# Two output weights prepared earlier, in other tiles, and the first gated values loaded ahead

## The chip, the cores and the metric

The kernel runs on one core of a Trainium2 chip, in one launch. The metric is the device time in microseconds (us), the median over runs. Times of single instructions and waits come from one execution that the hardware profiler recorded; times on its clock are counted from the start of its span.

## The reference

The program computes a decoder of two layers on a sequence of 1024 rows of 1024 numbers, all in float32. One layer reads its input once, mixes it in two parallel branches, and adds the result to the input:

```python
h = layer_norm(x) * (1 + scale) + shift        # scale, shift, gate from the condition
u, v, z_a, q, k, val, z_b, q_idx, k_idx, w_idx = split(h @ w_in)
y_a = silu(z_a) * spatial_gating_unit(u, v)    # 512 columns: the top half
y_b = silu(z_b) * sparse_attention(...)        # 512 columns: the bottom half
y = concatenate([y_a, y_b]) @ w_out
x = layer_norm(ALPHA * x + gate * y, ln_g, ln_b)
```

The attention has 8 heads of 64 and one shared key and value; an indexer scores all earlier keys of a query, and the softmax goes over the best 256 of them.

## The kernel before

The two layers run one after the other. In a layer the normalised input is laid out transposed (features on partitions), and split into a high and a low part. The two parts are 16 tiles of the pool "h" (128 x 1024 each): eight for the first half of the rows and eight for the second. A projection of 128 output columns and 512 rows is 24 matmuls (line 358): eight slices of the input, each as high times high, high times low, low times high. The layer does its projections in pairs, in an order that the list `specs` gives: indexer queries, v, q, then u, z_a, u, z_a, and last z_b twice. The gated values of the first branch, y_a, are made in four tiles of the pool "ya" (lines 501 to 504) and stored in DRAM when their second z_a projection is done. The z_b projections go to DRAM as zs (lines 514 and 515). Beside the projections VectorE (DVE) selects the keys.

After the last projection come the weights of the output projection. `load_wout` prepares 512 rows of w_out (part 0 is the top half, for y_a, part 1 the bottom half, for y_b), in four slices. Each slice is 512 KB that goes through one of two tiles "wr":

```python
nc.sync.dma_start(raw, ...)                     # line 728, SP
tensor_tensor(raw, raw, gate, op=ALU.mult)      # line 729, DVE or POOL
nc.scalar.activation(hi, raw, AF.Copy)          # line 731, ACT
tensor_tensor(lo, raw, hi, op=ALU.subtract)     # line 732, POOL or DVE
```

The high and low parts lie in tiles "h" as well, so a slice's results can be written only when the last projection has read the input that lay there. The raw tile is free for the next load when the low part is done.

Then comes attention in 16 steps, a step being 4 heads of one block of 128 queries. `att_soft` forms the scores (line 685), the running maximum and masked scores on DVE (686), the exponential on ACT (691) and the scaling on POOL (694); `att_pv` transposes the probabilities (705), splits them (708, 709) and multiplies them by the values (710, 711). Probabilities lie in tiles of "ya" and "w", which `PTAGS` names in turn. Between these steps other work is fitted in by a count of instructions: `out_top` loads an x row and a block of y_a (`load_top`, whose load is line 109 and whose split into high and low is lines 311 on ACT and 312 on POOL) and multiplies it by the top weights (line 747). `merge_top` does so when the bottom half is computed with it, and `out_bottom` adds the bottom half, the layer norm and the store.

The order in which instructions are issued on each engine is fixed when the program is built: a scheduler with a timeline of its own puts them in order, and on the chip each engine takes its instructions strictly in that order and waits for the semaphores of each. SP's order is the order in which loads and stores are issued. The scheduler can move a later instruction of an engine ahead of an earlier one, so what stands next to what can't be told from the source alone.

What the steps below touch: `load_wout` with its loads (728), products (729), copies (731) and subtractions (732); `out_top` and `load_top` with lines 109, 311 and 312; the last of the `specs`; `PTAGS`; and the TensorE line 747. In the changed kernel the same lines stand one or two further down (358 is 359, 311 is 312, 685 is 686, 728 is 730, 731 is 733, 747 is 749).

## Time and profile before

| | |
|---|---|
| median of three runs | 1181.41 us (1180.64 to 1185.3) |
| profiled execution, its own time | 1184.14 us |
| its span | 1182.4 us |
| mean granted TensorE clock | 0.977 |
| PE busy | 1109.5 us, 94% of the span |
| DVE busy | 838.2 us, 71% |
| POOL busy | 575.8 us, 49% |
| ACT busy | 512.2 us, 43% |

The profiled execution is 1.74 us longer than its span. The page's busy shares are means over stages that have different limits: PE's projections, stages where DVE is the fuller engine, and short stretches in which every engine waits. Where the time goes in one place is read from the timeline of that place, which gives for each group of instructions its start, its length, and, in brackets, the idle time of the engine before it and what ended it. The granted clock is a share of full speed, 1.00 being 2.4 GHz.

### The profile page before, as it was taken

Reading aid. Unit: us, or ns where it says so; the run is one execution under the profiler, and the core shown is the slowest. Engines: PE = TensorE matmul, PEld = TensorE weight load, DVE = VectorE, ACT = ScalarE, POOL = GpSimd, SP = SyncE. Lnnn points to the kernel's source line nnn. Section 1 sums busy time; section 2 is a strip of 40 time slices with the busy share of each in tenths; the row PEclk is TensorE's granted clock in tenths of the full one; section 3 lists DMA queues with packets and bytes.
Section 4 is the critical chain, followed back from the end, with each engine's and each line's share of the span. In section 5 each row is a group of like instructions: output and inputs, shape, how many; then the busy total and the mean of one; then the engine's idle time right before and its main releaser. Section 6 shows DMA issues by size and latency. Waiting matters only on the chain.

```text
span 1182.4 us, 16568 instructions
## 1 busy us (share of the span) xinstructions
PE 1109.5 (94%) x5460; PEld 883.6 (75%) x5460; DVE 838.2 (71%) x1884; ACT 512.2 (43%) x988; POOL 575.8 (49%) x485
## 2 busy tenths in 40 slices
PE   5889999999989799989988999999999989999997
PEld 0468888777768688867666788888778877787885
DVE  6775757889869356689975447579985737878775
ACT  0343555221122445466764526552222146667561
POOL 1464311566432666365766532114654457565653
PEclk9989999999989799999998999999999999999999
DMA  8935420378742664331322453213724345132311
GB/s 260 286 94 160 142 72 26 127 244 237 228 130 81 204 188 143 108 99 63 99 89 73 116 152 121 58 57 114 249 90 152 98 141 198 54 102 78 117 36 63
DMA packets 127057, 152.11 MB, mean 129 GB/s; under 512 B 17396, under 2 KB 94580, under 8 KB 126968
## 3 DMA queue, kind: packets, MB, share of 16 engines
q1 hardware_dynamic: 126968, 151.03, 40.5%
q8 instruction: 43, 0.70, 0.2%
q14 instruction: 46, 0.38, 0.1%
HBM read 111.40 MB, written 35.40 MB: 124 GB/s over the span
## 4 chain that ended last, share of the span: by engine, by line
PE 53%; DVE 8%; DMA 3%; issue 2%; POOL 2%; ACT 1%; SPq 0%; DVEq 0%; ACTq 0%; POOLq 0%
PE pacc L358 22%; PE pacc L747 14%; PE ps L685 4%; PE ppt L705 4%; PE po L711 3%; PE po L710 2%; PE ppt L535 2%; PE ps L535 1%; POOL h L732 1%; DVE ga L709 1%; DVE ya L686 1%; DVE w L686 1%; PE po L451 1%; DMA gc<-ya 1%; DVE gb L717 1%
## 5 line engine op out<-in xcount | busy, mean ns | idle before, releaser
L358 PE MATMUL pacc<-h,w 128*128 128x512 f32 (+2 forms) x2304 | 542.5, 389 | 6.9 <-ACT gc L501 6.4
L358 PEld LDWEIGHTS pacc<-h,w 128*128 128x128 f32 (+1 forms) x2304 | 420.0, 187 | 103.0 <-ACT gc L501 10.1
L312 POOL TENSOR_TENSOR w<-wr,w 128x512 fp32r<-128x512 f32 (+1 forms) x100 | 135.0, 1366 | 211.7 <-ACT w L311 203.0
L747 PE MATMUL pacc<-h,gc 128*128 128x512 f32 x768 | 199.6, 405 | 13.4 <-ACT gc L311 12.1
L747 PEld LDWEIGHTS pacc<-h,gc 128*128 128x128 f32 x768 | 145.1, 194 | 43.3 <-ACT gc L311 13.0
L542 DVE SCALAR_TENSOR_TENSOR sc<-gc,wi,sc 128x384 f32<-128x384 f32 (+3 forms) x140 | 97.4, 740 | 56.6 <-ACT gc L537 54.0
L311 ACT ACTIVATE w<-wr 128x512 fp32r<-128x512 f32 (+1 forms) x100 | 56.8, 602 | 154.4 <-PE pacc L358 95.0
L709 DVE TENSOR_TENSOR ga<-ppt,ga 128x512 fp32r<-128x512 f32 x144 | 97.0, 684 | 20.7 <-ACT ga L708 20.1
L685 PE MATMUL ps<-kd,q 128*128 128x512 f32 (+4 forms) x384 | 104.1, 368 | 7.1 <-DVE mx L686 6.5
L708 ACT ACTIVATE ga<-ppt 128x512 fp32r<-128x512 f32 x144 | 82.7, 592 | 38.6 <-PE ppt L705 37.9
L377 POOL TENSOR_TENSOR ga<-ga,ga 128x512 fp32r<-128x512 f32 (+2 forms) x40 | 52.7, 1324 | 83.6 <-ACT ga L376 80.4
L685 PEld LDWEIGHTS ps<-kd,q 128*128 128x128 f32 x384 | 64.2, 192 | 23.8 <-DVE mx L686 17.4
L694 POOL TENSOR_SCALAR w<-w,rd 128x256 f32<-128x256 f32 (+6 forms) x77 | 61.4, 801 | 40.8 <-DVE rd L693 24.4
L691 ACT ACTIVATE w<-w,mx 128x256 f32<-128x256 f32 (+6 forms) x77 | 60.6, 787 | 35.5 <-DVE mx L686 34.9
L705 PE MATMUL ppt<-ident,w 128*128 128x128 f32 x349 | 74.1, 275 | 0.5 <-POOL w L694 0.5
L248 POOL TENSOR_TENSOR rs<-rs,mhalf 128x1 f32<-128x1 f32 x48 | 30.2, 638 | 86.4 <-DVE rs L247 85.8
L710 PE MATMUL po<-ga,vv 128*128 128x512 f32 x144 | 61.9, 430 | 9.1 <-DVE gb L717 5.7
L550 DVE TENSOR_SCALAR_CACHE_REDUCE junkd<-sc,sv 128x384 int8<-128x384 f32 (+2 forms) x72 | 67.8, 942 | 1.7
L711 PE MATMUL po<-ga,vv 128*128 128x512 f32 x144 | 63.1, 438 | 4.1 <-DVE ga L709 3.9
L694 POOL TENSOR_SCALAR ya<-ya,rd 128x256 f32<-128x256 f32 (+6 forms) x51 | 40.8, 801 | 52.3 <-DVE rd L693 30.4
L537 ACT ACTIVATE gc<-ppt 128x384 f32<-128x384 f32 (+3 forms) x96 | 47.8, 526 | 40.2 <-PE ppt L535 35.8
L705 PE MATMUL ppt<-ident,ya 128*128 128x128 f32 x227 | 58.0, 275 | 1.4 <-DVE modT L235 1.4
(197 smaller groups left out, 1729.9 us busy)
## 6 DMA issues: line engine op xcount, KB each, us to landing
wr<-in_w_in SPq DMA_DIRECT2D x50, 512.0 KB, 4.4
r<-in_w_ada SPq DMA_DIRECT2D x32, 512.0 KB, 4.7
q<-q SPq DMA_DIRECT2D x112, 128.0 KB, 3.2
q<-ga SPq DMA_DIRECT2D x48, 256.0 KB, 2.2
h<-in_w_ada SPq DMA_DIRECT2D x32, 256.0 KB, 4.8
wr<-in_w_out SPq DMA_DIRECT2D x16, 512.0 KB, 4.1
r<-r SPq DMA_DIRECT2D x14, 512.0 KB, 3.6
r<-x SPq DMA_DIRECT2D x12, 512.0 KB, 4.5
```

The costliest lines, as they stand in the source:

```text
L312: self.nc.gpsimd.tensor_tensor(lo, src, hi.bitcast(F32), op=ALU.subtract)
L358: self.nc.tensor.matmul(acc[:m, :tn], w[:, k, :m], h[:, k % 2, t0:t0 + tn], start=(k == 0 and i == 0), stop=(k == NK - 1 and i == 2))
L542: nc.vector.scalar_tensor_tensor(sc[:, c0:c0 + w], r[:, :w], wsc, sc[:, c0:c0 + w], op0=ALU.mult, op1=ALU.add)
L550: self.nc.vector.tensor_scalar(j[:, :n], sc, thr, None, op0=op, op1=ALU.add, accum_out=out)
L685: self.last_pe = nc.tensor.matmul(ps[:, :w], q[:, g * 4 + h, :], self.KD[x][:, c0:c0 + w], start=(x == 0), stop=(x == 1)).ins
L694: nc.gpsimd.tensor_scalar(pm[:, :n], pm[:, :n], rd, 0.0, op0=ALU.mult, op1=ALU.add)
L705: nc.tensor.transpose(pt[:, h * P:(h + 1) * P], pr[h][:, kt * P:(kt + 1) * P], self.ident)
L708: nc.scalar.activation(ph, pt, AF.Copy)
L709: nc.vector.tensor_tensor(pl, pt, ph.bitcast(F32), op=ALU.subtract)
L710: nc.tensor.matmul(o, self.V[:, kt, :], ph, start=(kt == 0), stop=False)
L711: nc.tensor.matmul(o, self.V[:, kt, :], pl, start=False, stop=(kt == i))
L747: self.nc.tensor.matmul(acc, s[:, k, :], m[:, cs], start=(first and k == i == 0), stop=(not more and k == 3 and i == 2))
```

## The change

`load_wout` puts the first two slices of the top half into tiles "ya", and its first two rounds are asked for during the last projection pair. The remaining two and the bottom half stay in "h". In exchange two of five probabilities lie in "h" instead of "ya", except for the late steps of layer 0, which keep "ya". The x row and the block of y_a of the first `out_top` are loaded just ahead of the remaining weights. The call of `ada_step` that is removed had a count of zero.

```diff
--- before.py
+++ after.py
@@ -70,7 +70,8 @@
     PACE_SEL = 1.4
     PACE = 1.5
     STEPS = 6
-    PTAGS = ('ya', 'w', 'w', 'ya', 'w')
+    PTAGS = ('h', 'w', 'w', 'h', 'w')
+    PTAGS2 = ('ya', 'w', 'w', 'ya', 'w')
     ORDERS = ((1, 0, 2, 3, 4, 5, 6, 7), (4, 5, 6, 2, 3, 7, 1, 0))
     RDVE = 1
     DMOD = ()
@@ -676,7 +677,7 @@
         n = ch[-1][0] + ch[-1][1]
         pr = []
         for h in range(4):
-            pm = self.u(self.PTAGS[self.pcnt % len(self.PTAGS)])
+            pm = self.u(A["tags"][self.pcnt % len(self.PTAGS)])
             self.pcnt += 1
             mx = self.col("mx", 8, 2)
             for ci, (c0, w) in enumerate(ch):
@@ -724,10 +725,11 @@
         gate = self.u("r")
         nc.sync.dma_start(gate, self.gate_dram[l][0].partition_broadcast(P))
         for k in range(4):
+            tag = "h" if part or k > 1 else "ya"
             raw = self.u("wr")
             nc.sync.dma_start(raw, self.a["w_out"][l, part * 512 + k * P:part * 512 + (k + 1) * P, :])
             (nc.vector if k in self.WOD[part] else nc.gpsimd).tensor_tensor(raw, raw, gate, op=ALU.mult)
-            hi, lo = self.u("h", dt=F32R), self.u("h", dt=F32R)
+            hi, lo = self.u(tag, dt=F32R), self.u(tag, dt=F32R)
             nc.scalar.activation(hi, raw, AF.Copy)
             (nc.vector if k in self.WOL[part] else nc.gpsimd).tensor_tensor(lo, raw, hi.bitcast(F32), op=ALU.subtract)
             dst.append((hi, lo))
@@ -758,8 +760,7 @@
     def out_top(self, l, i, w):
         nc = self.nc
         rows = slice(i * P, (i + 1) * P)
-        x = self.load_row(self.xin[l], i)
-        y = self.load_top(l, i)
+        x, y = self.pre.pop(i, None) or (self.load_row(self.xin[l], i), self.load_top(l, i))
         for nh in range(2):
             acc = yield from self.out_mm(w, y, nh)
             xs = x[:, nh * 512:(nh + 1) * 512]
@@ -927,14 +928,16 @@
                 if n >= self.BACK:
                     ada_step(1)
 
+        wt, wb = [], []
+        top = self.load_wout(l, 0, wt)
         w = self.load_pair(l, specs[0][0], specs[0][1])
         for n, (c0, rope, f) in enumerate(specs):
             nw = self.load_pair(l, specs[n + 1][0], specs[n + 1][1]) if n + 1 < len(specs) else None
             for _ in f(w):
                 if n > 2:
                     side()
-                if n < self.BACK:
-                    ada_step(self.ADA1)
+                if n + 1 == len(specs) and len(wt) < 2:
+                    next(top)
             w = nw
             if n == 0:
                 for i in range(2, NB):
@@ -949,8 +952,9 @@
         for g in gens + back:
             self.drain(g)
         self.mark = {}
-        wt, wb = [], []
-        self.drain(self.load_wout(l, 0, wt))
+        first_top = self.ORDERS[l][self.TOPS[l].index(0)]
+        self.pre = {first_top: (self.load_row(self.xin[l], first_top), self.load_top(l, first_top))}
+        self.drain(top)
         bottom = self.load_wout(l, 1, wb)
         self.lg, self.lb = self.u("r"), self.u("r")
         nc.sync.dma_start(self.lg, a["ln_g"][l].partition_broadcast(P))
@@ -991,6 +995,7 @@
                 i, g = steps[t]
                 if g == 0:
                     A[i] = self.att_begin(l, i, masks[i])
+                A[i]["tags"] = self.PTAGS if last or t < 9 else self.PTAGS2
                 self.att_soft(A[i], g, fill)
                 if t == 0:
                     self.mark["pe"] = self.last_pe
```

Three places show what the scheduler made of it. The first is ACT at layer 0's junction, where the projections end. `h` and `ya` on the left of an L731 or L733 are high parts of weights, `gc<-pacc` are projections taken out of PSUM, and `gc<-gc` (L311, L312) is the first y's high part. Before:

```order
L514 ACTIVATE gc_4799<-pacc_4774 128x512
L731 ACTIVATE h_4914<-wr_4911 128x1024
L731 ACTIVATE h_4921<-wr_4918 128x1024
L514 ACTIVATE gc_4837<-pacc_4812 128x512
L731 ACTIVATE h_4928<-wr_4925 128x1024
L514 ACTIVATE gc_4878<-pacc_4853 128x512
L731 ACTIVATE h_4935<-wr_4932 128x1024
L514 ACTIVATE gc_4906<-pacc_4881 128x512
L691 ACT_TABLE_LOAD
L691 ACTIVATE ya_5025,den_5037<-ya_5025,mx_5026 128x256
L311 ACTIVATE gc_4975<-gc_4976 128x512
```

After:

```order
L733 ACTIVATE ya_4817<-wr_4814 128x1024
L733 ACTIVATE ya_4865<-wr_4862 128x1024
L515 ACTIVATE gc_4799<-pacc_4774 128x512
L733 ACTIVATE h_4935<-wr_4932 128x1024
L515 ACTIVATE gc_4846<-pacc_4821 128x512
L733 ACTIVATE h_4942<-wr_4939 128x1024
L515 ACTIVATE gc_4894<-pacc_4869 128x512
L733 ACTIVATE h_4955<-wr_4952 128x1024
L515 ACTIVATE gc_4922<-pacc_4897 128x512
L733 ACTIVATE h_4962<-wr_4959 128x1024
L312 ACTIVATE gc_4927<-gc_4928 128x512
L692 ACT_TABLE_LOAD
L692 ACTIVATE h_4974,den_4984<-h_4974,mx_4975 128x256
```

In the changed kernel the high part of the first y follows the copies of six weights, of which the last two, h_4955 and h_4962, are bottom weights; before it followed four copies and an exponential. The exponentials that ran before the first weights come behind it.

The second place is SP there. `wr<-in_w_out` is a load of weights, `gc<-ya` that of y, `zs<-gc` a store of z_b, `r<-gate` a load of the gate. Before:

```order
L728 DMA wr_4925<-in_w_out 128x1024
L515 DMA zs_92<-gc_4837 128x512
L728 DMA wr_4932<-in_w_out 128x1024
L668 DMA gb_4964<-zs_92 128x4x128
L306 DMA r_4973<-in_x 128x1024
L515 DMA zs_92<-gc_4878 128x512
L728 DMA wr_4945<-in_w_out 128x1024
L728 DMA wr_4952<-in_w_out 128x1024
L109 DMA gc_4976<-ya_94 128x4x128
L515 DMA zs_92<-gc_4906 128x512
```

After:

```order
L730 DMA wr_4932<-in_w_out 128x1024
L516 DMA zs_92<-gc_4799 128x512
L730 DMA wr_4939<-in_w_out 128x1024
L516 DMA zs_92<-gc_4846 128x512
L726 DMA r_4950<-gate_98 128x1024
L669 DMA gb_4971<-zs_92 128x4x128
L730 DMA wr_4952<-in_w_out 128x1024
L730 DMA wr_4959<-in_w_out 128x1024
L516 DMA zs_92<-gc_4894 128x512
L110 DMA gc_4928<-ya_94 128x4x128
L516 DMA zs_92<-gc_4922 128x512
```

The first y's load (gc_4976 before, gc_4928 after) still follows the loads of two bottom weights; in between, the second gate row is new.

The third place is PE at layer 1's junction, from the end of the projections. `ps` are scores, `ppt` transposes, `pacc` with `gc` on the right the output projection. Before (the first rows that are shown follow the last projection and three transposes):

```order
L685 MATMUL ps_12146<-kd_7725,q_12089 128x320
L685 MATMUL ps_12146<-kd_7726,q_12089 128x320
L685 MATMUL ps_12153<-kd_7725,q_12089 128x320
L685 MATMUL ps_12153<-kd_7726,q_12089 128x320
L685 MATMUL ps_12169<-kd_7725,q_12089 128x320
L685 MATMUL ps_12169<-kd_7726,q_12089 128x320
L685 MATMUL ps_12176<-kd_7725,q_12089 128x320
L685 MATMUL ps_12176<-kd_7726,q_12089 128x320
L685 MATMUL ps_12202<-kd_7725,q_12089 128x320
L685 MATMUL ps_12202<-kd_7726,q_12089 128x320
L747 MATMUL pacc_12114<-h_12044,gc_12109 128x512
L747 MATMUL pacc_12114<-h_12045,gc_12109 128x512
```

After, from the same transposes on:

```order
L749 MATMUL pacc_12114<-ya_11950,gc_12057 128x512
L749 MATMUL pacc_12114<-ya_11951,gc_12057 128x512
L749 MATMUL pacc_12158<-ya_11950,gc_12057 128x512
L749 MATMUL pacc_12158<-ya_11951,gc_12057 128x512
L686 MATMUL ps_12146<-kd_7725,q_12096 128x320
L686 MATMUL ps_12146<-kd_7726,q_12096 128x320
L749 MATMUL pacc_12114<-ya_11950,gc_12058 128x512
L749 MATMUL pacc_12114<-ya_11995,gc_12057 128x512
```

Ten score matmuls, ps_12146 to ps_12202, stood before the first output matmul and now come behind its first four and the later ones.

## Rows read from the trace of the kernel before

**Rows 1.** The page, chain that ended last: shares of the span by engine and line.

```profile
PE pacc L358 22%; PE pacc L747 14%; PE ps L685 4%; PE ppt L705 4%; PE po L711 3%; PE po L710 2%; PE ppt L535 2%; PE ps L535 1%; POOL h L732 1%; DVE ga L709 1%; DVE ya L686 1%; DVE w L686 1%; PE po L451 1%; DMA gc<-ya 1%; DVE gb L717 1%
```

**Rows 2.** Waits of PE: waited for, us in total, times, longest us.

```profile
PE pacc L747 <- ACT gc L311: 12.1, 3, 5.1
```

**Rows 3.** Timeline of PE, layer 0: start us, us, what, count, idle before and releaser.

```profile
389.66 7.19 PE L358 MATMUL pacc<-h,w 128*128 128x512 f32 x31
...
396.92 2.74 PE L233 MATMUL ppt<-ones,r 128*128 128x1 f32 x24
399.52 0.72 PE L685 MATMUL ps<-kd,q 128*128 128x256 f32 x4
400.07 1.51 PE L233 MATMUL ppt<-ones,r 128*128 128x1 f32 x8
...
408.37 2.07 PE L747 MATMUL pacc<-h,gc 128*128 128x512 f32 x4 [4.51 <-ACT gc L311]
...
413.64 6.56 PE L747 MATMUL pacc<-h,gc 128*128 128x512 f32 x20 [1.27 <-POOL gc L312]
...
422.23 5.71 PE L747 MATMUL pacc<-h,gc 128*128 128x512 f32 x24
```

**Rows 4.** Windows: busy us (count) of PE, PEld, DVE, ACT, POOL; clock; DMA share; GB/s.

```profile
396.85:408.37 11.52, 5.64 (x41) 5.15 (x40) 3.70 (x11) 4.11 (x7) 6.77 (x4) 0.65 0.70 233
408.37:420.20 11.83, 10.55 (x35) 8.39 (x36) 7.25 (x15) 7.03 (x15) 11.83 (x10) 0.62 0.74 216
420.20:440.00 19.80, 19.80 (x100) 16.60 (x100) 9.74 (x31) 8.45 (x21) 12.46 (x12) 1.00 0.64 215
...
540.00:580.00 40.00, 36.59 (x189) 27.81 (x187) 38.11 (x101) 27.38 (x53) 25.31 (x23) 1.00 0.23 76
```

**Rows 5.** Timeline of PE, layer 1's junction.

```profile
969.72 1.71 PE L685 MATMUL ps<-kd,q 128*128 128x320 f32 x6
971.63 0.97 PE L685 MATMUL ps<-kd,q 128*128 128x320 f32 x4 [0.21 <-DVE mx L686]
977.69 2.07 PE L747 MATMUL pacc<-h,gc 128*128 128x512 f32 x4 [5.09 <-ACT gc L311]
...
980.60 4.73 PE L747 MATMUL pacc<-h,gc 128*128 128x512 f32 x20
```

**Rows 6.** Timeline of SP, layer 0's junction.

```profile
400.09 2.95 SPq L728 DMA_DIRECT2D wr<-in_w_out  x2
403.10 0.43 SPq L109 DMA_DIRECT2D gc<-ya  x1
```

**Rows 7.** Timeline of ACT, layer 0's junction.

```profile
385.33 2.00 ACT L731 ACTIVATE h<-wr 128x1024 fp32r<-128x1024 f32 x2
...
407.69 0.63 ACT L311 ACTIVATE gc<-gc 128x512 fp32r<-128x512 f32 x1 [5.04 <-issue]
```

**Rows 8.** Timelines of POOL and DVE, layer 0's junction.

```profile
386.47 4.75 POOL L732 TENSOR_TENSOR h<-wr,h 128x1024 fp32r<-128x1024 f32 x2 [2.09 <-ACT h L731]
...
405.19 4.67 POOL L729 TENSOR_TENSOR wr<-wr,r 128x1024 f32<-128x1024 f32 x2 [2.50 <-DMA wr<-in_w_out]
...
380.84 1.21 DVE L729 TENSOR_TENSOR wr<-wr,r 128x1024 f32<-128x1024 f32 x1
...
396.56 2.61 DVE L729 TENSOR_TENSOR wr<-wr,r 128x1024 f32<-128x1024 f32 x1 [2.02 <-DMA gb<-zs]
```

**Rows 9.** Line 728, the loads of output weights: their time to landing.

```profile
DMA to landing us min/median/max: 3.4/4.1/5.7
```

**Rows 10.** Timelines of POOL, DVE and ACT, layer 1's junction.

```profile
949.24 2.40 POOL L729 TENSOR_TENSOR wr<-wr,r 128x1024 f32<-128x1024 f32 x1 [4.56 <-issue]
951.62 0.81 POOL L694 TENSOR_SCALAR w<-w,rd 128x640 f32<-128x640 f32 x1
...
964.64 3.29 DVE L729 TENSOR_TENSOR wr<-wr,r 128x1024 f32<-128x1024 f32 x1 [1.36 <-DMA wr<-in_w_out]
...
977.02 0.61 ACT L311 ACTIVATE gc<-gc 128x512 fp32r<-128x512 f32 x1
```

## Prediction

> **What bounds the kernel now.** I read the page's chain first, then PE's waits, then the timelines of the two places where those waits lie. The chain by line [rows 1] is TensorE's work: the projections (L358) hold 22% of the span and the output projection (L747) 14%; no other line holds more than 4%. A change that leaves the matmuls alone can win only where PE idles or runs at its lower clock. PE's waits put 12.1 us on one cause: L747 waiting for ACT's line 311, the high half of a block's gated values y, three times, 5.1 us the longest [rows 2]. The timeline shows the two large ones, one in each layer, where the projections end and the output projection begins. I call these places the junctions.
>
> Layer 0's junction: the last projection ends at 389.66 + 7.19 = 396.85; the small matmuls L233 and L685 follow; then PE waits 4.51 us and runs its first four L747 at 408.37, the next twenty at 413.64 after 1.27 us more [rows 3]. The windows give the granted clock: 0.65 and 0.62 up to 420.20, then 1.00 with PE busy without a gap [rows 4]; of the clock's two levels this is 1.2 GHz for the greater part, after an idle stretch. Four L747 took 2.07 us there, 0.52 each, and 24 of them 5.71 us after it, 0.24 each [rows 3]. Work in the 23.35 us from 396.85 to 420.20 at full clock: 24 L747 at 0.238 = 5.7, 32 L233 at 2.74/24 = 3.65, ten L685 and eight L705 at about 0.14 (four L685 start 0.55 us ahead of what follows them) = 2.5, together 11.9. **The junction loses 11.5 us.** Layer 1's first L747 stands at 977.69 after 5.09 us of waiting; the twenty at 980.60 run at full clock, 4.73/20 = 0.24 [rows 5].
>
> Why y's high half is late in layer 0: SP issues the load of y at 403.10, behind the weight loads of 400.09 [rows 6]; ACT converts it at 407.69 [rows 7]. The weights come through two "wr" tiles: a tile is loaded, multiplied by the gate, copied (high half, ACT), subtracted (low half), and only then free for the next load. That rotation is the clock of the junction.
>
> **The change, part by part.** It neither adds nor removes a matmul, a weight load or a conversion of weights. It moves the first two top pairs from tiles "h", which the last projection reads, into tiles "ya", which are free earlier; it moves y's first load and an x row ahead; it renames the tiles of two probabilities in five.
>
> *Weights, layer 0.* The chain starts with DVE's product at 380.84, which follows the key selection without idle time [rows 8], so it cannot start earlier. Then: product to 382.05, ACT's two copies at 2.00/2 [rows 7], the first done at 383.05, POOL's two subtractions at 4.75/2 = 2.37 [rows 8], done at 385.4 and 387.8. Before, they ended at 386.47 + 4.75 = 391.2, held by the "h" tiles and the exponentials on ACT: **3.4 us gained here**. Third and fourth tile: loads from 385.4 and 387.8. The median to landing is 4.1, from 3.4 to 5.7 [rows 9], so the fourth lands at 391.9; its product on DVE runs beside POOL's subtraction of the third, as at 396.56, 2.61 us [rows 8]: 394.5; copy 395.5; subtraction 397.9.
>
> *What is now ahead of y.* The rows of ACT's order show it: y's high half stood behind the four top pairs; now it stands behind these and two bottom weights. The second bottom weight needs the fourth top weight's tile: load issued at 397.9. The nearest load, that of 400.09, let POOL start at 405.19 [rows 6, 8], 5.1 us; I take this, since the DMA share there is 0.70 [rows 4] and the after has a gate, gate values and y in flight at that time. It lands at 403.0; POOL's product 4.67/2 = 2.33, 405.3; copy 1.0, 406.3; y's high half 0.63 [rows 7], **406.9, first L747 about 407.0**. y itself, issued behind that load and landing with the 4.6 us that separate 403.10 from 407.69, is there at 403; it waits for the ACT queue. Shortest: 387.8 + 3.4 + 1.21 + 1.0 + 2.37 + 3.4 + 2.33 + 1.0 + 0.63 = 403.1; longest, with 5.7 twice and 3.29 [rows 10]: 409.8.
>
> *What PE does meanwhile.* In the new order nothing stands between PE's last projection and that first L747; the L233 and L685 that filled 396.85 to 404 before are behind it. PE then idles from the projections' end to 407.0, 10.15 us in all; ACT's evacuation of a projection behind the third weight's copy may stall the last projection by a microsecond, but that shifts the idle and adds none. After it PE need not wait again (y's low half is one subtraction on POOL, with matmuls to fill). Half-clock time: in layer 1 it lasted at most from 977.69 to 980.60, 2.9 us, costing 1.4; in layer 0 the twenty L747 took 6.56 against 4.76. I take layer 1's, where PE did not wait again either. Loss after: 10.15 + 1.4 = 11.55 against 11.5. **Layer 0: 0.0 us**, from -3.9 to +2.8 by the two ends, and +1.8 where the clock stays low as before.
>
> *Layer 1*, same steps: POOL's product 949.24 + 2.40 = 951.64, subtraction 2.37 → 954.0, a probability 0.81 → 954.8, subtraction → 957.2 [rows 10]. Load 4.1 → 961.3; product beside POOL 3.29 → 964.6; copy 965.6; subtraction 968.0; load 4.1 → 972.1 (the median [rows 9]); product 974.5; copy 975.5; y 0.61 → 976.1. Before: 977.02 + 0.61, first L747 at 977.69. So 1.5 us earlier, from 972.6 to 979.3 by the same ends. But ten L685 that ran ahead of it (six in 1.71, four in 0.97 [rows 5]) now come behind: 10 at 0.15 = 1.5 us. **Layer 1: 0.0 us**, -3.5 to +3.2.
>
> *The rest.* The probability tiles in "h" carry no new work; a probability needs "h" tiles freed by the projection, which is over. The softmax that stood early goes behind the junction; PE is the engine without a gap from 420.20 to 440 with DVE at 9.74 of 19.80 us [rows 4], so DVE has room. From 540 to 580 DVE is the fuller engine, 38.11 of 40 us with PE at 36.59 [rows 4], and a gain in layer 0 can be partly swallowed there. The gate row, the x row and the order of SP cost nothing while the DMA share of 0.64 to 0.74 [rows 4] leaves room.
>
> The trace has a product of 2.61 and of 3.29 us beside POOL against 1.21 without. In the Trainium skill the GPSIMD Engine Reference (Specifications) says that POOL shares its SBUF interfaces with VectorE and that they contend when a VectorE instruction has two SBUF inputs; the product has two, and the trace agrees. By the uncontended time each chain would be 1.4 or 2.1 us shorter, so the rule speaks against this change, which puts product and subtraction side by side.
>
> **Sum.** 0.0 + 0.0 on the profile's own 1184.14 us, which is 2.7 (0.2%) above the median of 1181.41: at the median 1181.
>
> **The rivals.** *The wait goes (faster).* Each load of the chain lands in 3.4 us and product and subtraction do not meet; first L747 at 403.1 and 972.6. Then -3.9 - 3.5 = -7.4, at the median 1174; if the clock then does not fall in layer 1, 1.4 more: 1172.6. For it: the first pairs are ready 3.4 us earlier, and y is in place by 403. Against it: 3.4 is the shortest of 16 loads, and ACT's order keeps y behind the last of them. The Trainium skill's page DMA: Bandwidth & Descriptors (Rules for kernel authors) says to issue a load early and wait late, so that its cost is hidden; by that rule alone the first L749 would follow y's landing at 403. No row of before shows it, since y was loaded last there.
>
> *y queues behind bottom weights (slower).* In both layers ACT's copy of y waits for a bottom weight that the before did not need so early. If that weight's load lands 5.7 us after its issue, twice in a chain, PE idles until 409.8 and 979.3: +2.8 + 3.2 = +6.0, 1187.4; and 1.8 more if layer 0's clock stays low as before: 1189.2. It decides from a fourth weight's landing in layer 0 later than about 393 and a second bottom weight's later than 404. For it: 5.1 is already the row at that place. Against: 4.1 is the median.
>
> *The change does nothing where it counts*, because the rotation of two "wr" tiles and not the room for results limits it, or because DVE swallows the gain later: 1180 to 1182. This lies with the forecast.
>
> **How the numbers follow.** About 0.5%, 5.9 us, is what a measurement of this kernel can tell from no change. Forecast with the third rival (within it): 0.47. The wait goes: 0.29; 5.9 us are most of the way to both shortest ends, and the chance is that high because the product's contention and the second load are the two terms I know least. Slower: 0.24. The range reaches from 1172 (first rival with the clock) to 1189 (second, with the clock) and leaves out the rest.
>
> **What would show it.** Right: in the changed profile PE waits for ACT's line 312 for about 9 us before its first L749 in layer 0, which starts near 407; ACT does two weight copies just ahead of the conversion of y; the first L749 of layer 1 near 976, and the ten L686 behind it. The "ya" copies near 382 to 384 and 949 to 953, and the third top load issued near 385.4 instead of 388.9, show the early part right. Wrong: a first L749 before 404 (y not held by ACT's queue), a granted clock of 1.00 through a junction, or PE's time after 420 differing by more than 2 us.

## The result and the profile after

The changed kernel takes 1188.61 us (median of 12 runs, 1184.69 to 1194.03), the kernel before 1181.08 (12 runs beside them, 1178.98 to 1190.24). The ratio is 1.0054, with the interval 1.0033 to 1.0075: 0.5% slower, about 6.4 us (the medians alone lie 7.5 us apart), where the forecast was no change. The profiled execution took 1185.83 us, its span is 1184.1.

The chain that ended last answers to [rows 1]:

```profile
PE pacc L359 36%; PE pacc L749 14%; PE ps L686 4%; PE ppt L706 4%; PE ppt L536 3%; PE po L712 2%; PE ps L536 2%; DMA r<-in_w_ada 2%; PE po L711 2%; DVE r L201 1%; DVE ga L710 1%; PE po L452 1%; DVE w L687 1%; DMA h<-in_w_ada 1%; DVE junkd L551 1%
```

The projections hold 36% instead of 22% only because the chain was followed back by another path: their busy time is 544.0 us in all, and was 542.5. A chain's shares compare causes inside one execution, not sizes between two. The waits of PE say more (waited for, total, times, longest), against 12.1, 3 and 5.1 in [rows 2]:

```profile
PE pacc L749 <- ACT gc L312: 17.6, 3, 8.8
...
PE ps L686 <- DVE mx L687: 7.8, 20, 1.1
```

The wait for y's high half grew by 5.5 us: by 4.3 in layer 0, as the prediction said it would, and by 1.1 in layer 1, which it did not say. PE's timeline at layer 0's junction, against [rows 3]:

```profile
392.82 5.73 PE L359 MATMUL pacc<-h,w 128*128 128x512 f32 x24 [1.59 <-ACT gc L515]
407.40 2.08 PE L749 MATMUL pacc<-ya,gc 128*128 128x512 f32 x4 [8.85 <-ACT gc L312]
409.28 1.05 PE L686 MATMUL ps<-kd,q 128*128 128x256 f32 x4
410.13 3.41 PE L234 MATMUL ppt<-ones,r 128*128 128x1 f32 x16
413.40 2.05 PE L749 MATMUL pacc<-ya,gc 128*128 128x512 f32 x4
```

From 398.55 to 407.40 PE has nothing to do. The scores (L686) and the narrow L234 that filled this stretch before now come behind the first four output matmuls, and at the lower clock: an L749 takes 0.52 us, sixteen L234 3.41. The window of these six microseconds (columns as in [rows 4]) has PE busy throughout and a granted clock of 0.50:

```profile
407.40:413.40 6.00, 6.00 (x25) 5.62 (x25) 2.63 (x13) 4.60 (x11) 4.73 (x4) 0.50 0.67 218
```

ACT and SP, against [rows 7] and [rows 6]:

```profile
391.23 1.06 ACT L733 ACTIVATE h<-wr 128x1024 fp32r<-128x1024 f32 x1 [6.52 <-DVE wr L731]
...
403.38 1.06 ACT L733 ACTIVATE h<-wr 128x1024 fp32r<-128x1024 f32 x1 [8.33 <-POOL wr L731]
...
405.77 1.06 ACT L733 ACTIVATE h<-wr 128x1024 fp32r<-128x1024 f32 x1 [0.85 <-POOL wr L731]
406.74 0.61 ACT L312 ACTIVATE gc<-gc 128x512 fp32r<-128x512 f32 x1
```

```profile
385.79 0.33 SPq L730 DMA_DIRECT2D wr<-in_w_out  x1
...
388.14 0.33 SPq L730 DMA_DIRECT2D wr<-in_w_out  x1
...
395.77 2.69 SPq L730 DMA_DIRECT2D wr<-in_w_out  x2
398.55 0.38 SPq L516 DMA_DIRECT2D zs<-gc  x1
398.98 0.43 SPq L110 DMA_DIRECT2D gc<-ya  x1
```

y's load is issued 4.1 us earlier than before (398.98, not 403.10) and wins 0.95 us for its conversion (406.74, not 407.69), because ACT's queue keeps that behind two bottom weights, whose products POOL makes one after the other from 401.01. The row of 395.77 holds two loads, one for each of them; the second, seen alone, went out at 398.12. POOL's row follows it:

```profile
398.12 0.33 SPq L730 DMA_DIRECT2D wr<-in_w_out  x1
...
401.01 4.73 POOL L731 TENSOR_TENSOR wr<-wr,r 128x1024 f32<-128x1024 f32 x2 [2.92 <-DMA wr<-in_w_out]
```

Layer 1, PE first, against [rows 5], then DVE:

```profile
967.20 0.49 PE L706 MATMUL ppt<-ident,w 128*128 128x128 f32 x3
973.90 2.07 PE L749 MATMUL pacc<-ya,gc 128*128 128x512 f32 x4 [6.21 <-ACT gc L312]
975.77 0.73 PE L686 MATMUL ps<-kd,q 128*128 128x320 f32 x2
```

```profile
968.81 1.23 DVE L734 TENSOR_TENSOR h<-wr,h 128x1024 fp32r<-128x1024 f32 x1 [7.04 <-ACT h L733]
973.36 1.23 DVE L734 TENSOR_TENSOR h<-wr,h 128x1024 fp32r<-128x1024 f32 x1 [3.32 <-ACT h L733]
974.50 0.48 DVE L687 CUSTOM_DVE_ANT_0 h<-ps,sc 128x320 f32<-128x320 f32 x1
```

The same stretch of DVE in the kernel before:

```profile
969.16 0.49 DVE L686 CUSTOM_DVE_ANT_0 ya<-ps,sc 128x320 f32<-128x320 f32 x1 [1.22 <-PE ps L685]
...
971.49 0.49 DVE L686 CUSTOM_DVE_ANT_0 w<-ps,sc 128x320 f32<-128x320 f32 x1
...
974.91 1.23 DVE L732 TENSOR_TENSOR h<-wr,h 128x1024 fp32r<-128x1024 f32 x1 [2.93 <-ACT h L731]
976.06 0.55 DVE L686 CUSTOM_DVE_ANT_0 w<-ps,sc,mx 128x320 f32<-128x320 f32 x1
```

Here is what the prediction passed over. Before, softmaxes (L686 on DVE) ran while PE waited for y; a part of the attention's chain came free. After, the first of these (L687) stands at 974.50, 7.7 us behind the end of the projections (966.78), where it stood 0.33 us behind it (968.83). In layer 0 it is the same. Before, a row of DVE in that wait is

```profile
402.89 0.41 DVE L686 CUSTOM_DVE_ANT_0 w<-ps,mask 128x256 f32<-128x256 f32 x1
```

and three of step 0's four softmaxes had run at 328.69, 381.98 and 382.32, during the projections; after, the first of all is

```profile
408.00 0.42 DVE L687 CUSTOM_DVE_ANT_0 h<-ps,mask 128x256 f32<-128x256 f32 x1
```

The cause is a tile. The first probability of step 0 (in layer 1 the second: the first lies in "w" in both kernels and runs during the projections, at 948.51 before and 946.50 after) now lies in an "h" tile, and the projections' input holds those until the last projection has read it. The scheduler puts step 0's softmaxes from there on behind subtractions of weights on DVE (404.47 in layer 0, 973.36 in layer 1), and the scores that follow behind the first four output matmuls on PE. The kernel below that gives step 0 other tiles has them ahead again.

To see what this costs, both kernels were traced twice, and three of the kernels below (one layer's half of the change each, and the change without its early calls) have one of the two orders. PE's loss is its idle time plus its busy time times (1 - granted clock), added over windows of 1 us; layer 0's stage runs from its last projection's end to layer 1's first projection.

| stretch: idle + low clock in us | order as before | order as after |
|---|---|---|
| layer 0, first 24 us | 7.15+4.96, 6.28+3.72, 7.01+3.31 | 8.84+4.50, 9.22+1.66, 10.01+4.72, 9.97+5.98 |
| layer 0, behind the first 104 us | 16.85+6.73, 16.31+3.02, 15.36+3.19 | 14.15+4.64, 14.31+8.19, 14.12+3.10, 14.11+6.37 |
| layer 0's stage | 25.10+11.68, 23.70+6.74, 23.48+6.51 | 24.09+9.15, 24.98+9.85, 25.24+7.82, 25.19+12.35 |
| its length | 242.92, 237.89, 236.92 | 239.15, 240.56, 239.00, 243.20 |
| layer 1, from the projections' end to the kernel's end | 17.81+1.43, 17.69+2.05, 17.95+2.00 | 20.39+2.86, 19.81+1.43, 20.10+2.09, 20.39+2.03 |
| its length | 213.57, 214.16, 214.44 | 217.32, 215.38, 216.24, 216.49 |

(As before: before, its second trace, and the kernel changed in the other layer alone. As after: after, its second trace, the kernel without early calls, the kernel changed in this layer alone.) Layer 1 is 2.3 us longer (216.36 against 214.06 in the mean), in every execution, and PE's idle time there is 2.35 us longer. Layer 0's junction idles 2.7 us more (9.51 against 6.81), but its late attention 2.0 less, so the stage has only 0.8 us more idle time; its low clock goes from 6.5 to 12.4 us by the execution, in either order, and hides what smaller difference there may be. The stage begins at the projections' end, so the table leaves out the stall ahead of it: in the order as after the last projection waits for ACT, 1.59, 1.20, 1.19 and 1.34 us in the four executions, and in the order as before not at all. With these 1.3 us layer 0 is 2.6 us longer in the mean, from lengths that differ by 4 to 6 us within one order. The windows show the stretches: columns as in [rows 4]; 30 us from 6 us ahead of layer 0's projections' end, the late attention, and layer 1 from 24 to 64 us behind its projections; first the kernel before (its second trace), then the changed one.

```profile
391.98:421.98 30.00, 23.73 (x119) 19.91 (x118) 13.41 (x29) 13.18 (x23) 20.45 (x14) 0.77 0.70 228
...
501.98:635.87 133.89, 117.59 (x607) 90.19 (x605) 110.94 (x293) 88.92 (x167) 92.48 (x79) 0.97 0.29 89
988.94:1028.94 40.00, 38.88 (x206) 31.25 (x205) 32.32 (x98) 25.98 (x49) 19.90 (x21) 1.00 0.32 107
```

```profile
392.55:422.55 30.00, 20.88 (x92) 17.90 (x93) 10.19 (x24) 10.07 (x19) 20.80 (x12) 0.77 0.57 183
...
502.55:637.70 135.15, 121.02 (x623) 94.11 (x621) 112.51 (x292) 89.68 (x168) 90.60 (x77) 0.96 0.28 88
...
990.78:1030.78 40.00, 37.80 (x202) 30.52 (x203) 34.38 (x110) 30.18 (x58) 22.05 (x23) 1.00 0.33 98
```

In layer 0's junction PE does 2.85 us less, DVE 3.2 and ACT 3.1 us less, which come later; in layer 1 DVE and ACT have 2.1 and 4.2 us more to do in the 40 us behind it, and PE 1.1 us less.

Is it the clock? Every execution, traced or not, comes with its mean granted clock. The 80 timings of the kernel before that were made with the experiments lie on a line: 1181.64 us at 0.9773, and 0.65 us more for each 0.001 less (correlation -0.74). The changed kernel's 12 have a mean clock of 0.9759, which is worth 0.9 us; they lie 6.5 us above that line (standard error 0.5). So the clock explains about a seventh of the change. The line is the scatter of one kernel, and a kernel whose order changes the clock need not follow it: two of those below have a higher mean clock and lie 8 us above it.

### The profile page after: what moved, and what is told of

Read it like the earlier page. It is cut to its first block, busy times and chain, and to the rows that moved or that the text cites. A ratio compares the mean times of both kernels' runs of the same rounds, so it can differ in the third digit from the quotient of the medians.

```text
span 1184.1 us, 16577 instructions
## 1 busy us (share of the span) xinstructions
PE 1107.7 (94%) x5460; PEld 883.9 (75%) x5460; DVE 837.8 (71%) x1884; ACT 507.2 (43%) x984; POOL 576.3 (49%) x485
## 4 chain that ended last, share of the span: by engine, by line
PE 71%; DVE 11%; DMA 6%; issue 4%; POOL 3%; ACT 2%; SPq 2%; DVEq 0%; ACTq 0%; POOLq 0%
PE pacc L359 36%; PE pacc L749 14%; PE ps L686 4%; PE ppt L706 4%; PE ppt L536 3%; PE po L712 2%; PE ps L536 2%; DMA r<-in_w_ada 2%; PE po L711 2%; DVE r L201 1%; DVE ga L710 1%; PE po L452 1%; DVE w L687 1%; DMA h<-in_w_ada 1%; DVE junkd L551 1%
## 5 line engine op out<-in xcount | busy, mean ns | idle before, releaser
L359 PE MATMUL pacc<-h,w 128*128 128x512 f32 (+2 forms) x2304 | 544.0, 390 | 8.8 <-ACT gc L502 6.8
L749 PE MATMUL pacc<-h,gc 128*128 128x512 f32 x576 | 151.4, 402 | 2.6 <-ACT gc L312 2.5
L312 ACT ACTIVATE w<-wr 128x512 fp32r<-128x512 f32 (+1 forms) x100 | 57.0, 602 | 166.8 <-PE pacc L359 102.5
L749 PEld LDWEIGHTS pacc<-h,gc 128*128 128x128 f32 x576 | 109.1, 193 | 25.0 <-ACT gc L312 3.2
L686 PE MATMUL ps<-kd,q 128*128 128x512 f32 (+4 forms) x384 | 100.8, 365 | 8.4 <-DVE mx L687 7.8
L686 PEld LDWEIGHTS ps<-kd,q 128*128 128x128 f32 x384 | 64.0, 191 | 23.4 <-DVE mx L687 17.3
L749 PE MATMUL pacc<-ya,gc 128*128 128x512 f32 x192 | 56.8, 419 | 15.1 <-ACT gc L312 15.1
L503 POOL TENSOR_TENSOR ya<-ya,gc 128x512 f32<-128x512 f32 x32 | 48.4, 1519 | 22.0 <-ACT gc L502 18.3
```

Of the source, the lines that this page charges most:

```text
L359: self.nc.tensor.matmul(acc[:m, :tn], w[:, k, :m], h[:, k % 2, t0:t0 + tn], start=(k == 0 and i == 0), stop=(k == NK - 1 and i == 2))
L686: self.last_pe = nc.tensor.matmul(ps[:, :w], q[:, g * 4 + h, :], self.KD[x][:, c0:c0 + w], start=(x == 0), stop=(x == 1)).ins
L749: self.nc.tensor.matmul(acc, s[:, k, :], m[:, cs], start=(first and k == i == 0), stop=(not more and k == 3 and i == 2))
```

## The experiments

Two theories stood at first: the tiles and the order they bring cost the time (through the fill that moved, or through the clock it lowers), or the early call and load do, by what they put into the queues. Diffs are against the changed kernel where nothing else is said.

**Without the early calls.**

```diff
-                if n + 1 == len(specs) and len(wt) < 2:
-                    next(top)
...
-        self.pre = {first_top: (self.load_row(self.xin[l], first_top), self.load_top(l, first_top))}
+        self.pre = {}
```

> The change with two of its parts taken out: the first two top weights are prepared after the last projection in the program's text, not during it, and the first y and x row are not loaded ahead; the tiles (ya for two top pairs, h for two of five probabilities) stay changed. On every engine the order around both junctions comes out as in the changed kernel. Theory A (the tiles alone make the difference, the early call and the early load do nothing): ratio to before 1.003 to 1.008, first L749 near 407 and 974. Theory B (the early load's traffic or the early preparation costs the time): ratio within 0.2% of 1, and a first L749 a few us away from 407.

Measured: 1188.42 us, 1.0057 [1.0038, 1.0076], the changed kernel's ratio. The order around the junction is the same, and the early call and the early load make no difference that can be told; the tiles bring the new order and the time.

**The first y in a tile of its own, loaded and split during the last projections.** In `load_top`, and asked for in the loop over the last projection:

```diff
+        if tag == "r":
+            yr = self.u("r", (P, 2, 4, P), F32R)
+            y = yr[:, 0], yr[:, 1]
...
+                elif n + 1 == len(specs) and not self.pre:
+                    first_top = self.ORDERS[l][self.TOPS[l].index(0)]
+                    self.pre = {first_top: (self.load_row(self.xin[l], first_top), self.load_top(l, first_top, "r"))}
```

> The changed kernel with the first y loaded into a tile of the pool r during the last projections, so that its high and low half stand on ACT and POOL ahead of all output weights. Theory A (PE loses its time to the wait for ACT's conversion of y behind the bottom weights, and to the low clock after it): the waits of 8.85 and 6.21 us and most of the half-clock time (5.7 and 3.5 us) go, ratio to before 0.985 to 0.992 (10 to 18 us faster than before). Rival C (the score matmuls and the softmax that come behind the output projection cost the time, so that VectorE is late in the attention): the waits go, yet the ratio stays at 0.996 or above, and the time comes back as waits of PE for VectorE before 580 and before 1060.

Measured: 1186.22, 1.0037 [1.0020, 1.0053], as rival C had it and not theory A. PE's timeline:

```profile
397.92 1.52 PE L749 MATMUL pacc<-ya,r 128*128 128x512 f32 x6
...
405.29 0.73 PE L749 MATMUL pacc<-ya,gc 128*128 128x512 f32 x2 [1.77 <-ACT gc L312]
...
416.51 1.97 PE L749 MATMUL pacc<-ya,gc 128*128 128x512 f32 x6 [2.98 <-DVE r L771]
...
423.66 0.64 PE L686 MATMUL ps<-kd,q 128*128 128x256 f32 x4
```

The wait is gone: the first L749 follows the projections at once. But some seventy output matmuls now run ahead of the first scores, at 423.66, and the late attention idles 17.18 us, where the changed kernel has 14.1 to 14.3. Over layer 0's stage PE idles 23.95 us and loses 8.55 to the clock: as much as with the wait. What the junction gives, the attention takes. That output matmuls which are spent early are missing as fill later is the reading that fits; no run tests it alone.

**Useless matmuls in the wait**, 40 in layer 0 and 28 in layer 1 between the last projection and the first output matmul, in the changed kernel and in the one before:

```diff
+        o = self.p("acc")
+        for k in range((40, 28)[l]):
+            nc.tensor.matmul(o, self.V[:, 0, :], self.V[:, 0:4, :], start=True, stop=True)
```

> The changed kernel with 40 (layer 0) and 28 (layer 1) matmuls of no use between the last projection and the first L749, 128x512 each on the values tile, about 9 and 6 us of PE at full clock, into a PSUM tile that is not read. They only fill the wait. Theory A (low clock after the wait is a main term, 5.7 us and 3.5 us against 3.5 and 1.4 in the kernel before): granted clock 1.00 through both junctions, ratio to the kernel before 0.995 to 1.000, so 5 to 9 us faster than the changed kernel. Rival C (order of the work, not the clock): no faster than the changed kernel, 1.004 to 1.008.

> The kernel before with the same matmuls of no use in the same place; the score matmuls that ran in the wait come behind them. Theory A (clock): the 3 to 5 us that the low clock costs in the kernel before come back, less what the fill that is now behind costs (2.5 + 3.65 us in layer 0 and 1.5 us in layer 1): ratio 0.998 to 1.005. Rival C (fill behind the output projection delays the softmax and VectorE): slower by 4 us or more, 1.004 to 1.010.

Measured: 1197.67, 1.0142 [1.0120, 1.0164], and 1193.64, 1.0106 [1.0087, 1.0126]. The first is slower than both theories had it, the second is just above rival C's range, which its interval reaches. In the changed kernel:

```profile
395.76 9.23 PE L957 MATMUL pacc<-vv 128*128 128x512 f32 x40
406.57 0.73 PE L749 MATMUL pacc<-ya,gc 128*128 128x512 f32 x2 [1.58 <-ACT gc L312]
...
410.16 0.40 PE L686 MATMUL ps<-kd,q 128*128 128x256 f32 x2
```

The 40 fit into the wait, with 1.58 us to spare, and keep the clock up: the first 24 us lose 2.70 + 1.38 instead of some 14. Yet layer 0's stage takes 251.05 us instead of 240.5 (mean of four), with 22.51 us of idle time, 18.69 of it late, and 13.02 of low clock. The stage is longer by 10.5 us, somewhat more than the 9.23 us of the useless work, so filling the wait at full clock gains nothing here: the idle time that it saves comes back late (18.69 against 14.2), and low clock with it. A price of a matmul can't be read from it: the scheduler ordered what follows differently too, as the scores behind nine L749 show.

**One layer alone**, 0, then 1. In each, the diff's edits are bound to `l == 0` or `l == 1`:

```diff
-            tag = "h" if part or k > 1 else "ya"
+            tag = "h" if part or k > 1 or l != 0 else "ya"
...
-                A[i]["tags"] = self.PTAGS if last or t < 9 else self.PTAGS2
+                A[i]["tags"] = self.PTAGS if l == 0 and (last or t < 9) else self.PTAGS2
```

> The change in layer 0 alone; layer 1 has the order of the kernel before, row for row. Profiles so far: layer 0 from its last projection to layer 1's first took 242.9 us before and 239.2 after, its last projections end 1.7 us later. By these rows: ratio 0.997 to 1.000 (0 to 3 us faster), so that layer 1 carries the whole loss. Rival D (the profile of before was a slow one of its kind in layer 0, and the late scores cost there too): ratio 1.002 to 1.005.

> The change in layer 1 alone; layer 0 has the order of the kernel before, row for row. Profiles so far: from layer 1's last projection to the end 213.6 us before and 217.3 after. By these rows: 3 to 5 us slower, ratio 1.0025 to 1.0045. Rival D (both layers lose about the same): ratio 1.002 to 1.003; if the loss is layer 0's alone, within 0.1% of 1.

Measured: 1185.84, 1.0038 [1.0022, 1.0053], and 1183.87, 1.0019 [0.9998, 1.0039]: 4.5 and 2.2 us, together 6.7, the whole of the change's 6.4. By the line of clock and time they are 3.9 and 2.7 (errors 0.5 and 0.7). Layer 1's share agrees with the 2.3 us of the table, though its ratio alone can't be told from 1. Layer 0's ratio is rival D's: the first profile's shorter stage (239.2 against 242.9) had misled.

**Both kernels traced again.**

> The kernel before once more, for a second profile: by rival D its layer 0 takes 239 to 241 us from the last projection to layer 1's first, less than the 242.9 of the first profile; if the first profile was typical, 242 to 244.

> The changed kernel once more, for a second profile: by rival D its layer 0 takes more than the 239.2 us of the first profile, 241 to 244; if the first profile was typical, 238 to 240.

Measured: 1180.77 and 1182.85 us, 3.4 and 3.0 below the first traces; layer 0's stage took 237.89 and 240.56 us, the one below both ranges, the other between them. The pairs of traces are 1.9 us apart in the mean, the medians 7.5: single traces scatter by half of the effect, and layer 0's stage by more than its share of it, so stages are compared over three or four of them above.

**Step 0's probabilities in "w" tiles**, which nothing holds there:

```diff
-                A[i]["tags"] = self.PTAGS if last or t < 9 else self.PTAGS2
+                A[i]["tags"] = ("w",) * 5 if t == 0 else self.PTAGS if last or t < 9 else self.PTAGS2
```

> The changed kernel, but the four probabilities of each layer's first half step lie in tiles w in place of h, which the last projection holds. With that alone the score matmuls, transposes and the small L234 stand ahead of the first L749 on PE again in both layers, as in the kernel before, and the first softmax is done during the projections; the top weights stay in ya. Theory F (the tile h of the first probabilities pushes the scores and the softmax behind the output projection's first block, so that they no longer run free inside the wait; 3 us in layer 0 and 2.3 us in layer 1 by the profiles): the loss goes, ratio to before 0.996 to 1.000, and PE's loss from 6 us before the end of layer 0's projections to 24 us after it falls from about 14 us to 10 or 11. Rival G (the rotation of the weights with more DVE and POOL work side by side, or the longer low clock, costs the time whatever stands in the wait): ratio 1.003 to 1.006.

Measured: 1183.04, 1.0023 [1.0005, 1.0041], between the ranges of theory F and rival G. PE's timeline:

```profile
387.32 11.18 PE L359 MATMUL pacc<-h,w 128*128 128x512 f32 x48 [2.51 <-ACT gc L515]
398.34 0.64 PE L686 MATMUL ps<-kd,q 128*128 128x256 f32 x4
398.81 2.74 PE L234 MATMUL ppt<-ones,r 128*128 128x1 f32 x24
406.79 1.22 PE L686 MATMUL ps<-kd,q 128*128 128x256 f32 x4 [5.24 <-DVE mx L687]
...
410.54 2.06 PE L749 MATMUL pacc<-ya,gc 128*128 128x512 f32 x4
```

Scores and L234 stand ahead of the first output matmul again, and although that is 3.1 us later than in the changed kernel, the kernel takes 0.3% less; layer 1's length from the projections to the end is back at 214.85. In layer 0 the first 24 us lose 8.5 us (5.24 idle and 3.22 of low clock); with the 2.51 us of stall ahead it is 11.0, as in the order before (10.8) and not as in the order after (13.7, with its stall 15.1). That is one execution. By its timings the kernel lies, at its clock, 2.3 us (error 0.7) above the line of the kernel before, where the changed kernel lies 6.5. Undoing this part alone takes back 0.31% of the 0.54%, with an uncertainty of 0.28% (the two half-widths, 0.21 and 0.18, combined), so that it takes back some of it is barely clear of noise, and how much is not known.

**Both: y in its own tile and step 0 in "w".**

> As the last one, with the first y loaded into a tile r during the projections, so that neither y nor the first softmax waits. Theory F with the wait gone: both junctions lose less than 5 us in place of 11 and 7, and if nothing is given back later the ratio is 0.990 to 0.995. Rival H (output matmuls done early are missed as filler in the attention, where VectorE is the fuller engine, so PE's idle time there grows by as much): ratio 0.998 to 1.003, with PE's idle time from 104 us after the projections to the end of layer 0 above 16 us.

Measured: 1186.6, 1.0056 [1.0035, 1.0077]. The junction of layer 0 loses 0.42 us in 30, and the next 80 us lose 11.4:

```profile
395.56:425.56 30.00, 29.59 (x155) 24.64 (x153) 9.31 (x22) 9.88 (x17) 14.42 (x9) 1.00 0.76 235
425.56:505.56 80.00, 72.82 (x340) 59.65 (x341) 50.58 (x156) 39.92 (x93) 45.26 (x48) 0.94 0.46 133
```

```profile
427.65 0.85 PE L686 MATMUL ps<-kd,q 128*128 128x256 f32 x4 [2.26 <-DVE mx L687]
...
438.06 0.98 PE L686 MATMUL ps<-kd,q 128*128 128x384 f32 x2 [3.86 <-DMA q<-q]
```

With the output matmuls spent, PE waits for the softmax and for a query load instead; over the stage it idles 24.34 us, as in the others. Its mean clock is the higher for it, 0.981, and it is no quicker. The ratio is above the ranges of both theories; rival H's sign came, 16.78 us of idle time from 104 us behind the projections. The expected sum of two gains did not come.

**The third and fourth weight's copies on DVE**, to keep the last projection's evacuation on ACT from waiting; on top of step 0 in "w", then on the changed kernel alone:

```diff
-            nc.scalar.activation(hi, raw, AF.Copy)
+            if part or k < 2:
+                nc.scalar.activation(hi, raw, AF.Copy)
+            else:
+                nc.vector.tensor_copy(hi, raw)
```

> As the kernel with step 0's probabilities in w, and the high parts of the third and fourth top weight are copied by VectorE and not by ACT, so that no projection waits on ACT behind a weight's copy. Theory F with the stall as its second part (the last projection waits 1.3 to 2.5 us for ACT's evacuation queued behind the third weight's copy): the stall goes and the ratio falls from 1.0023 to 0.998 to 1.001. Rival (the stall only shifts the wait for the weights, as the prediction had it): ratio unchanged, 1.001 to 1.004.

> The changed kernel, with nothing changed but that copy of the third and fourth top weight on VectorE. Stall as a cost of its own: ratio 1.002 to 1.004 in place of 1.0055. Stall only shifts the wait: 1.0045 to 1.007, with no wait of a projection for ACT's line 517 in the profile and the first output matmul still about 9 to 11 us behind the last projection.

Measured: 1187.15, 1.0034 [1.0010, 1.0059], and 1185.69, 1.0043 [1.0020, 1.0067]. The first didn't do what it was for: 2.73 us of stall stayed in the projections, behind exponentials that moved up on ACT. The second did; PE's timeline there:

```profile
383.70 9.46 PE L359 MATMUL pacc<-h,w 128*128 128x512 f32 x41
404.21 2.08 PE L752 MATMUL pacc<-ya,gc 128*128 128x512 f32 x4 [11.06 <-ACT gc L312]
```

The projections end 393.15 without a stall, and the wait is 11.06 us instead of 8.85: a stall ahead of a wait for something else only moves the wait. This kernel's time lies between the two ranges and can't be told from the changed kernel's. The first lies 5.2 us above the line at its clock, so with the copies moved little is left of what step 0's tiles gave back; why, no run shows. No version beat the kernel before.

## Why the prediction was wrong

*The chain of weights: right.* Third and fourth load predicted at 385.4 and 387.8, issued at 385.79 and 388.14; end of y's high half and first L749 406.9 and 407.0, measured 407.35 and 407.40; nine microseconds of waiting there, measured 8.85. The second bottom weight's load went out at 398.12 (predicted 397.9), its product started at 403.40 (predicted 403.0), in between it landed, at 403.26, after the 5.1 us that were taken for it. One part was right by two errors, the product and the subtraction beside each other (below). In layer 1 the first L749 was to come 7.3 us behind the projections' end, and came 7.1 behind it; on the clock it stands at 973.90 and not near 976, because the projections end 2.05 us earlier in this execution.

*The stall that shifts the idle and adds none: right*, by the kernel with copies on DVE: stall and idle time together are 10.4 to 11.3 us in four executions with the stall, and 11.06 without it.

*Layer 0, the term that failed: "Half-clock time ... I take layer 1's", 1.4 us.* PE's idle time was nearly foreseen: 10.15 in all, and 10.4 to 11.3 in four executions with the stall ahead, 10.8 in the mean. But the low clock cost 4.50, 1.66, 4.72 and 5.98, 4.2 in the mean, and in the order before 4.96, 3.72 and 3.31, 4.0. The sum rested on trading more idle time for less low clock; the idle time came (+4.0, of it 1.3 in the stall), the trade didn't. The junction measured +4.2 (15.1 with the stall, against 10.8) and not 0.0: 2.8 of this is the low clock, 0.7 the longer idle time, and 0.7 that the order before lost 10.8 in the mean of three and not 11.5. The text had +1.8 for a clock that stays low and did not take it. Behind the junction the stage gives back part of this, 2.0 us of idle time late in the attention, which the prediction did not foresee either.

*Layer 1 and "DVE has room": failed.* The ten scores were priced by PE's time, 1.5 us, and set against a first L749 1.5 us earlier; behind the projections it does come 1.7 us earlier (7.12 after 8.86). But nothing fills PE's wait any more, which grows from 5.1 to 6.1 us (means of three and four executions). And softmaxes hang on the scores, which in the wait had been free: from there to the end PE's scores wait 4.05 us for DVE's running maximum (L687), where they waited 2.03, as DVE and ACT have the moved work to do. Other waits are shorter by 0.7, and 2.35 us of idle time remain as the loss. DVE had room in the row that I read, 420 to 440; the question was whether the chain of scores, softmax and transposes had, and that starts 7.7 us behind the projections where it had started at once.

*"y queues behind bottom weights", the slower rival:* its mechanism (ACT's order) is the forecast's own and was there, but its price was a late landing, and none landed late. The time that it gave, 1187.4 to 1189.2, is met for another reason. *"The wait goes"* was brought about in two kernels, and neither was faster (1.0037, 1.0056): taking away PE's wait was worth nothing here. So the rival's price of -7.4 us was wrong too. By the Trainium skill's page DMA: Bandwidth & Descriptors (Rules for kernel authors) the fixed setup cost of a DMA that is issued early overlaps with compute (the setup cost, and not all of its cost, as the prediction put it); the trace agrees as to the wait (first L749 at 397.92), and the time is no shorter.

*Product and subtraction beside each other:* of the Trainium skill's GPSIMD Engine Reference (Specifications) it had been said that its contention speaks against the change. In layer 0 POOL paid, not DVE:

```profile
392.25 1.23 DVE L731 TENSOR_TENSOR wr<-wr,r 128x1024 f32<-128x1024 f32 x1 [1.12 <-DMA wr<-in_w_out]
...
392.36 5.74 POOL L734 TENSOR_TENSOR h<-wr,h 128x1024 fp32r<-128x1024 f32 x2 [4.24 <-ACT h L733]
```

The product took 1.23 us, as alone, and not 2.61; the two subtractions took 5.74 us instead of 4.76, 3.38 the first of them, so the second began 1.1 us behind its copy. The fourth weight was done at 398.10 (predicted 397.9): the two errors cancel. In layer 1 DVE paid: its product at 958.93 began behind POOL's subtraction of 958.30 and took 2.84 us.

*What stays open.* Layer 1's 2.3 us are found. Layer 0 alone costs 4.5 us by timing (interval 2.6 to 6.3), 3.9 at equal clock. The traces show +4.2 in its junction with the stall, but 2.6 over stall and stage together, within the scatter of the low clock there; where the rest lies is not settled. That the step-0 tiles carry a part is shown, by the ratio only just, by the kernel that undoes them; that it is the greater part (0.31 of 0.54%, or 4.2 of 6.5 us at equal clock) is the best estimate and not more. The converse, the kernel before with nothing but step 0's tiles changed, was not run. What remains with these tiles set right, 0.2%, isn't settled either: that kernel still has its top weights in "ya", later probabilities in "h" and a stall of 2.51 us in the last projection. The copies on DVE were to test that stall, and in that kernel 2.73 us of it stayed.

## What to carry to other kernels

Work that runs in a wait is free there and not behind it: before moving fill, price not its own engine's time but the chain that hangs on it, at the place where it lands. A wait that is taken away may gain nothing, if what follows needs as its fill the work that was waiting; look at where the same engine idles later. And a tile's name is an order: where a pool's tile is still held, the first to ask for it goes behind the holder, and all that depends on it, on every engine.

## What was not expected of the hardware

Of TensorE's low clock, one order of instructions had 4.50, 1.66, 4.72 and 5.98 us in the same 24 us, in four executions with 8.8 to 10.0 us of idle time there, and 7.8 to 12.4 over the stage. The lower level, 1.2 GHz, stayed while PE was busy: in the changed kernel the granted clock was 0.50 for 6.00 us in which PE was busy without a gap behind the wait (407.40 to 413.40), and four L749 at 413.40 still took 2.05 us; among what ran between were sixteen matmuls of one column, 3.41 us. In its second trace the four L749 behind the same sixteen took 1.18 us. In the kernel with useless matmuls, 9.23 us of 128x512 in place of the wait left 1.38 us of it.

DVE and POOL delay each other, and in these rows the one that starts second pays. DVE's product of 392.25 kept its 1.23 us and POOL's subtraction, begun at 392.36, took 3.38 instead of 2.4; in layer 1 POOL's subtraction of 958.30 kept its 2.40 us and DVE's product, begun at 958.93, took 2.84 instead of 1.2.
